# Closed groups of small products, an early split of branch A and sample rows on 128 partitions in a hybrid decoder step

## The chip, the cores and the metric

The kernel runs on one core of a Trainium2 chip. The metric is the device time of one execution in microseconds. Before the change three runs took 897.95, 898.17 and 901.1 us; the median is 898.17 us.

## The reference, cut to what matters

One inference step of a one-layer decoder, for a prompt of 512 rows and for 8 samples of 4 rows each (32 rows). The kernel treats them side by side: 544 columns of rows in all, of which the last 32 are the samples.

```
shift, scale, gate = split(silu(c) @ w_cond + b_cond)
h = x * (1 + scale) + shift
qa, ka, va, za, qkv_b, zb, a_b, b_b, g_a, g_b = split(h @ w_in)
yA = combine(dilated_attention(qa, ka, va, cache_kv, rel_bias)) * silu(za)
yB = rmsnorm(gated_delta(conv(qkv_b), a_b, b_b, state_delta)) * silu(zb)
merged = sigmoid(g_a) * (yA @ w_branch_a) + sigmoid(g_b) * (yB @ w_branch_b)
y = LayerNorm(ALPHA * x + gate * (merged @ w_out)) * ln_g + ln_b
```

Branch A has three head groups (windows 128, 512, 2048 with dilations 1, 4, 16); the samples also attend to caches of 2048 positions. Branch B is the delta rule with a 128x128 state per head, for the samples loaded from `state_delta`. All outputs are f32, the caches and states are returned too.

## The kernel before

Every large product is made in three passes: an operand is split in a rounded high part and the remainder (`hi` and `lo` of the weights, `hhi` and `hlo` of h, `yah` and `yal` of branch A), and hi by hi, lo by hi and hi by lo are summed in PSUM. ACT rounds the high part, DVE subtracts for the low part, PE multiplies. The rows go in two halves of 272 columns, so a job (`Job`: 128 output columns with 8 weight tiles) has 48 matmuls of 272 columns into the PSUM tile `pp`. `stream` runs the jobs one after the other: column jobs of `w_in`, gate jobs (`gate_job`), branch jobs (`branch_job`). The smaller work runs in threads beside it, in the PSUM tiles `pg`, `pd` and `pb`: prompt attention, the delta rule, the sample parts.

The instructions are not issued in the order of the code. A recorder collects them with their dependencies and plans an order for each engine: of what is ready by its cost model, the one with the lowest rank and number goes first; `.at` keeps an instruction back until a time; `rec.together()` makes a group that is issued without another PE instruction between its members, once the operands of all are there. The engines then run in that order. So an edit at one place can move instructions at many others. Each engine's queue is in order: an instruction that waits holds all behind it. SP issues all large DMAs, among them copies of the caches from memory to memory (`out_kv_s`), which stand between the loads.

All instructions are emitted from one line (L725), so the profile is read by names of tiles. The names that the change touches:

- Start: `cond_block` multiplies the conditioning weights `wc` with `cs` (eight products of 32 columns each), copies the sum (`Y`), and with `selc` brings it to features, which gives the scale `sc`. With it `x1h` and `x1l` are made from `xT`, and the first 272-column products (`x1h,hi`) start.
- Sample queries: `sample_queries` transposes the 64 columns of two groups of `qs` for a pair of tiles. T is 0 for the first half of the heads, 1 for the second.
- Sample attention: `sample_attention` makes scores of cache keys (`slab,Qz`; `kv,Qz` for T = 1) and new keys (`ks,Qz`) in `pg`, in products of 32 columns. Its bias comes by DMA as `bias_s` and is changed on ACT (`slab<-slab 128x352`). The same stretch of the program runs the delta rule of the prompt (`U`, `XF`, `W`, `NTs`, `vr`).
- Sample states: `sample_delta` loads for each group G of four heads the states S (8 samples, 512 KB a head) and multiplies each with keys and queries (`KP`), 64 products of 32 columns in a group, G = 0 into `pd` and G = 1 into `pb`. S0 to S3 are those of G = 0, S4 to S7 of G = 1.
- Branch A: `ya` holds attention times silu of za. Its sample columns are written last, by `gate_samples`, after the second sample attention (`od`, `om`, `o`, `os_`). After that the four tiles of 544 columns are split into `yah` and `yal`, and the branch jobs of A start.
- Output: `samples_out` multiplies the merged samples with `w_out` into four blocks of 32 partitions, moves them to one block of 32 rows by 1024 columns, and normalises there; `norm_out` does that for prompt tiles of 128 rows.

Of the kernel before, what the change touches and what calls it, by code (L numbers as in the profile page):

```python
# [19 lines left out]
D = 1024  # L20
# [20 lines left out]
S0B = 7  # L41
TOGETHER = ((0,), (1, 2), (3, 4), (5, 6), (7,))
CHUNKS = ((0, 1), (1, 1), (2, 2), (4, 2), (6, 2))

# [33 lines left out]
def shape_constants():  # L78
# [15 lines left out]
    blk["dmask_s"] = np.where(same & (p[:, None] <= p[None, :]), 0.0, -BIG)  # L94
    blk["bmask"] = (p[:, None] % 32 // 4 == np.arange(8)[None, :])
    blk["hmask"] = (p[:, None] % 4 == np.arange(4)[None, :])
    sab = np.zeros((128, 4, 4))
# [7 lines left out]
    for names in (("ident", "selc", "selg", "low16", "dmask"), ("selab", "sel16", "triu", "btri", "bones"),  # L105
                  ("strict4", "dmask_s", "bmask"), ("hmask",)):
# [671 lines left out]
def body(ctx, tc, io):  # L778
# [27 lines left out]
    def pb_():  # L806
        return psb.tile([128, 512], F32, name="pb", tag="b")
# [85 lines left out]
    with ExitStack() as fctx:  # L893
# [616 lines left out]
    def bias_table(j):  # L1510
# [4 lines left out]
        return bias  # L1515

    dw = dram.tile([2, 4, 2, 4, 128], F32, name="dw")

# [9 lines left out]
    def attention_job(j, g, s):  # L1528
# [4 lines left out]
        def evac(n, ps):  # L1533
            t, scale = pairs[j][s, g], 1.0 if s else -0.125
            if g == 0:
                lo, hi = ((0, 272), (272, 512))[n]
                se.activation(t[:, lo:hi], ps[:, 0:hi - lo], AF.Copy, scale=scale)
            else:
                v = t.rearrange("p (r a n) -> p n a r", r=4, a=4)
                m = (17, 15)[n]  # L1540
                se.activation(v[:, 17 * n:17 * n + m], ps[:, 0:16 * m].rearrange("p (n a r) -> p n a r", a=4, r=4),
                              AF.Copy, scale=scale)
            if n:
                se.activation((qs, ks, vs)[s][:, j, g, :], ps[:, 240:272], AF.Copy, scale=scale)
                if s == 2:
                    threads.set(ready[j, g], 2.5)
# [202 lines left out]
    def sample_attention(T, t, stream, W, pace_of, by, over):  # L1749
# [51 lines left out]
        pS = pg()  # L1801
        for jl in range(2):
            for x in range(1024 // W):
                kt = kts[jl, x]
                for bl in range(0, nb, 2):
                    b = nb * x + bl
                    pe.matmul(pS[16 * b:16 * b + 32, 0:256], Qz[:, 0, jl, 4 * b:4 * b + 8].rearrange("p i h -> p (i h)"),
                              kt[:, 128 * bl:128 * bl + 256], start=(jl == 0), stop=(jl == 1), tile_position=(0, 16 * b))
        for g in range(3):
            for jl in range(2):  # L1810
                for bp in range(4):
                    pe.matmul(pS[32 * bp:32 * bp + 32, 256 + 32 * g:288 + 32 * g],
                              Qz[:, g, jl, 8 * bp:8 * bp + 8].rearrange("p i h -> p (i h)"), ks[:, 2 * T + jl, g, :],
                              start=(jl == 0), stop=(jl == 1), tile_position=(0, 32 * bp))
        ve.tensor_tensor_reduce(Sa, pS[:, 0:352], sb["a"], 1.0, 3e38, op0=OP.add, op1=OP.min, accum_out=sst[:, 0:1])
# [88 lines left out]
    def sample_delta():  # L1904
# [34 lines left out]
        for G in range(2):  # L1939
# [10 lines left out]
            yield 12.0 if G else 6.0  # L1950
            for u in range(2):
                for b in range(8):
                    for h4 in range(4):
                        pe.matmul(pq[32 * h4:32 * h4 + 32, 128 * u:128 * u + 128],
                                  KP[:, u, h4, 32 * b:32 * b + 32], S0[h4][:, b, :],
                                  start=(b == 0), stop=(b == 7 and u == 0), tile_position=(0, 32 * h4))
            rr = rrs[G]
# [326 lines left out]
    ve.memset(eps5, LN_EPS)  # L2284
    r = [o1.tile([128, D], F32, name=f"r{tt}") for tt in range(5)]
    bn = [o1.tile([128, 4 if tt == 3 else 2, 6], F32, name=f"bn{tt}") for tt in range(5)]
# [11 lines left out]
    def load_x(tt, n):  # L2298
        rows = slice(0, 128) if tt < 4 else slice(0, 32)
        xr = o2.tile([128, 512], F32, name="xr")  # L2300
        sp.dma_start(xr[rows], io["x"][128 * tt:128 * tt + 128 if tt < 4 else NT, 512 * n:512 * n + 512])
        se.activation(xr[rows], xr[rows], AF.Copy, scale=ALPHA)
        return xr[rows]

    def norm_out(tt, mv=None):
        rows = slice(0, 128) if tt < 4 else slice(0, 32)
        q = r[tt][rows]
        if mv is None:
            mv = o2.tile([128, 4], F32, name="mv")[rows]
            ve.bn_aggr(mv[:, 0:2], bn[tt][rows].rearrange("p a b -> p (a b)"))  # L2310
        se.activation(mv[:, 2:3], mv[:, 1:2], AF.Sqrt, bias=eps5[rows, 0:1])
        ve.scalar_tensor_tensor(q, q, mv[:, 0:1], lng[rows], op0=OP.subtract, op1=OP.mult)
        ve.reciprocal(mv[:, 2:3], mv[:, 2:3])
        out = io["y_p"][128 * tt:128 * tt + 128] if tt < 4 else io["y_s"]
        for w in (slice(0, 512), slice(512, 1024)):
            ve.scalar_tensor_tensor(q[:, w], q[:, w], mv[:, 2:3], lnb[rows, w], op0=OP.mult, op1=OP.add)
            sp.dma_start(out[:, w], q[:, w])

    def samples_out():
        xr = [load_x(4, n) for n in range(2)]  # L2320
# [7 lines left out]
        q = r[4][0:32]  # L2328
        for b in range(4):
            rows = slice(32 * b, 32 * b + 32)  # L2330
            ve.scalar_tensor_tensor(q[:, 256 * b:256 * b + 256], po[rows, 0:256], 0.5, gs[rows], op0=OP.mult, op1=OP.mult)
        for n in range(2):
            w = slice(512 * n, 512 * n + 512)
            ve.tensor_add(q[:, w], q[:, w], xr[n])
            ve.bn_stats(bn[4][0:32, n, :], q[:, w])
        norm_out(4)

# [56 lines left out]
def lay_out(x):  # L2394
# [12 lines left out]
        "const_d": CONST[2],  # L2407
        "const_s": CONST[3],
        "x": rows,
        "xT": rows.T.reshape(KT, 128, NT).transpose(1, 0, 2),  # L2410
# [60 lines left out]
```

## Time and profile before

| | us |
|---|---|
| median of three runs | 898.17 |
| profiled execution, whole | 902.66 |
| its span | 900.9 |
| PE busy | 873.6 |
| DVE busy | 650.8 |
| ACT busy | 449.9 |
| POOL busy | 74.1 |

The mean granted clock of TensorE is 0.993. The queue of the large transfers is busy 76.3% of the span. Where rows of the profile or the timeline are shown, a tile's name is followed by what it is made of (`pp<-hhi,hi`: into `pp` from `hhi` and `hi`), PEld is the weight load that runs beside PE, SPq is the time in which SP issues a DMA, and `128*32` is the part of the array that a product uses (rows by columns). An f32 product that is not rounded runs in two passes and shows as two instructions.

### The profile page before, as it was taken

The page shows a single profiled execution, that of the slowest core. Times are in us where ns is not written, and L with a number is a line of the kernel's source. Part 1 is how long each engine was busy: PE and PEld are TensorE (multiplying, and loading weights), DVE is VectorE, ACT ScalarE, POOL GpSimd, SP SyncE. Part 2 cuts the span into 40 slices and gives each one's busy share as a digit, 9 for nine tenths or more (in the row PEclk, how much of TensorE's full clock was granted, in tenths as well). Part 3 has the DMA queues.
Part 4 walks back from the last instruction along what each step waited for, and adds up shares of the span by engine and source line. Part 5 has one row for each costly group of instructions (what it writes and reads, how often), then busy time and mean ns, then how long its engine had stood idle before and what let it go on. Part 6 is the DMA issues. An engine that isn't in the chain of part 4 may idle for free.

```text
span 900.9 us, 20727 instructions
## 1 busy us (share of the span) xinstructions
PE 873.6 (97%) x8178; PEld 822.2 (91%) x8178; DVE 650.8 (72%) x1341; ACT 449.9 (50%) x1076; POOL 74.1 (8%) x173
## 2 busy tenths in 40 slices
PE   6999999999999999999999999999999999989995
PEld 5899999898899999899999899897999999989884
DVE  3675447643379998399987658366889698978568
ACT  3555478733478834579734565642542222324331
POOL 0120011100101200012101101020010000001000
PEclk9999999999999999999999999999999999999998
DMA  9865785785868798878889556559869799985953
GB/s 348 322 212 172 235 277 174 249 275 165 293 200 302 234 293 276 309 245 261 274 287 286 188 193 214 177 180 317 315 224 382 270 408 411 352 305 170 366 187 122
DMA packets 106189, 235.84 MB, mean 262 GB/s; under 512 B 30199, under 2 KB 61633, under 8 KB 103405
## 3 DMA queue, kind: packets, MB, share of 16 engines
q1 hardware_dynamic: 106092, 234.53, 76.3%
q8 instruction: 64, 1.05, 0.5%
q14 instruction: 33, 0.26, 0.1%
HBM read 218.20 MB, written 103.97 MB: 358 GB/s over the span
## 4 chain that ended last, share of the span: by engine, by line
PE 83%; DVE 7%; ACT 4%; DMA 4%; issue 1%; SPq 1%; DVEq 0%; ACTq 0%
PE pp L725 63%; PE pg L725 9%; PE pd L725 7%; PE pb L725 4%; DVE slab L725 1%; ACT L725 1%; DMA S<-in_state_delta 1%; DVE lo L725 1%; DMA rbo<-dO 1%; DVE acc L725 1%; DVE r L725 1%; DMA slab<-in_bias_s 1%; SPq L725 1%; DMA out_kv_s<-in_cache 1%; DMA wc<-in_w_cb 1%
## 5 line engine op out<-in xcount | busy, mean ns | idle before, releaser
L725 PE MATMUL pp<-hhi,hi 128*128 128x272 f32 x1360 | 400.8, 295 | 1.0 <-DVE zt L725 0.5
L725 PE MATMUL pp<-hlo,hi 128*128 128x272 f32 x1360 | 400.8, 295 | 0.0
L725 PE MATMUL pp<-hhi,lo 128*128 128x272 f32 x1360 | 399.9, 294 | 0.0
L725 PEld LDWEIGHTS pp<-hhi,hi 128*128 128x128 f32 x1360 | 256.8, 189 | 4.8 <-issue 2.2
L725 PEld LDWEIGHTS pp<-hhi,lo 128*128 128x128 f32 x1360 | 256.6, 189 | 3.8 <-issue 2.7
L725 PEld LDWEIGHTS pp<-hlo,hi 128*128 128x128 f32 x1360 | 257.1, 189 | 2.8 <-issue 1.7
L725 ACT ACTIVATE hi<-wt 128x1024 fp32r<-128x1024 f32 (+1 forms) x101 | 103.6, 1026 | 160.3 <-PE pp L725 135.1
L725 DVE TENSOR_TENSOR lo<-wt,hi 128x1024 fp32r<-128x1024 f32 (+1 forms) x101 | 119.0, 1178 | 81.3 <-ACT hi L725 74.5
L725 DVE SCALAR_TENSOR_TENSOR acc<-ext,cw,acc 128x568 f32<-128x568 f32 x72 | 57.9, 804 | 0.8 <-ACT acc L725 0.2
L725 DVE TENSOR_TENSOR slab<-slab 128x512 f32<-128x512 f32 (+1 forms) x66 | 43.3, 670 | 10.0 <-DMA slab<-qd 4.4
L725 ACT ACT_TABLE_LOAD x32 | 41.1, 1283 | 5.2 <-PE pp L725 3.0
L725 DVE TENSOR_REDUCE slab<-slab 128x8 f32<-128x512 f32 (+2 forms) x66 | 42.8, 660 | 0.3
L725 ACT ACTIVATE zt<-pp 128x272 f32<-128x272 f32 x48 | 18.8, 391 | 40.6 <-PE pp L725 38.4
L725 ACT ACTIVATE P<-P,st 128x256 f32<-128x256 f32 (+1 forms) x64 | 31.3, 493 | 12.7 <-DVE st L725 12.6
L725 PE MATMUL pp<-ybh,lo 128*128 128x272 f32 x128 | 37.0, 289 | 0.0
L725 PE MATMUL pp<-ybl,hi 128*128 128x272 f32 x128 | 37.0, 289 | 0.0
L725 PE MATMUL pp<-ybh,hi 128*128 128x272 f32 x128 | 36.8, 288 | 0.0
L725 POOL COPY cx<-ext 128x3 f32<-128x3 f32 (+1 forms) x48 | 23.9, 527 | 114.5 <-ACT ext L725 109.9
L725 DVE CUSTOM_DVE_ANT_0 P<-pg,bias 128x256 f32<-128x256 f32 (+1 forms) x64 | 23.1, 401 | 9.3 <-PE pg L725 9.1
L725 ACT ACTIVATE spare<-pp 128x272 f32<-128x272 f32 (+1 forms) x32 | 16.2, 505 | 19.8 <-PE pp L725 18.2
L725 PEld LDWEIGHTS pp<-ybh,hi 128*128 128x128 f32 x128 | 24.2, 189 | 0.1
L725 PEld LDWEIGHTS pp<-ybl,hi 128*128 128x128 f32 x128 | 24.1, 188 | 0.1
(402 smaller groups left out, 1574.5 us busy)
## 6 DMA issues: line engine op xcount, KB each, us to landing
out_kv_s<-in_cache SPq DMA_DIRECT2D x144, 512.0 KB
wt<-in_w_in SPq DMA_DIRECT2D x85, 512.0 KB
out_kv_s<-in_cache SPq DMA_DIRECT2D x24, 496.0 KB
wc<-in_w_cb SPq DMA_DIRECT2D x16, 512.0 KB
slab<-in_ks SPq DMA_DIRECT2D x32, 256.0 KB
slab<-in_vs SPq DMA_DIRECT2D x32, 256.0 KB
kv<-in_ks SPq DMA_DIRECT2D x16, 512.0 KB
kv<-in_vs SPq DMA_DIRECT2D x16, 512.0 KB
```

What stands on the lines that cost most here:

```text
L725: getattr(real[x.engine], x.name)(*map(arg, x.args), **{k: arg(v) for k, v in x.kw.items()})
```

## The change

It has six parts.

1. At the start, `cond_block` for the first chunk of the scale issues products of `ones` with itself: 8 ahead of its group, 2 behind it, 5 behind the product with `selc`. Nothing reads them. The next chunk's group is kept back until 9.9 us.
2. The three groups of `qs` are stored in rotated order (`at_g`), so that the transposition takes 96 columns from the start of the tile; the first 64 rows of the result are used as before.
3. The scores of the first sample attention and the products of the states of G = 0 become closed groups.
4. The prompt columns of `ya` are split by a thread, `split_prompt_a`, which starts when the fourth job from the end of the gate jobs is over; at the border only the 32 sample columns are split, straight from `os_`.
5. The sample rows stay on 128 partitions (four blocks of 256 columns), with `ln_g` and `ln_b` loaded so (`lns`); the mean and the mean square over the four blocks come from two products with a constant matrix (`quarter`).
6. By all this the planned order differs in many places.

```diff
+IDLE = (8, 2, 5)
...
+    blk["quarter"] = np.where(p[:, None] % 32 == p[None, :] % 32, 0.25, 0.0)
...
+            idle = IDLE if (part, at) == (1, 0) else (0, 0, 0)
             rec.rank = -1
+
+            def turn_over(n):
+                for _ in range(n):
+                    pe.matmul(ps[:, 384:512], ones, ones, start=True, stop=True)
+
+            turn_over(idle[0])
             with rec.together():
                 for k in range(KT):
                     q = k % 4
                     pe.matmul(ps[32 * q:32 * q + 32, 0:w].rearrange("p (a b) -> p a b", b=128), cs[:, k, :], wc[:, :, k, :],
-                              start=(k < 4), stop=(k >= 4), tile_position=(0, 32 * q))
+                              start=(k < 4), stop=(k >= 4), tile_position=(0, 32 * q)).at = 9.9 * ((part, at) == (1, 1))
+                turn_over(idle[1])
...
+                turn_over(idle[2])
...
+    at_g = lambda g: (g + 2) % 3
...
-            pe.transpose(pt[0:64, 0:128], qs[:, 2 * T + jl, 1:3].rearrange("p g n -> p (g n)"), ident).at = GATES[1] + 12.0
+            pe.transpose(pt[0:96, 0:128], qs[:, 2 * T + jl].rearrange("p g n -> p (g n)"), ident).at = GATES[1] + 12.0
...
+        with rec.together() if not T else nullcontext():
...
         for j in range(4):
-            ve.tensor_copy(ya[j][:, SEQ:], os_[:, j])
+            se.activation(yah[j][:, SEQ:], os_[:, j], AF.Copy)
+            ve.tensor_sub(yal[j][:, SEQ:], os_[:, j], yah[j][:, SEQ:].bitcast(F32))
+
+    def split_prompt_a():
+        yield split_at.over
+        for j in range(4):
+            yah[j] = keep.tile([128, NT], F32R, name="yah", tag="ya", bufs=5)
+            se.activation(yah[j][:, :SEQ], ya[j][:, :SEQ], AF.Copy)
+            yal[j] = op.tile([128, NT], F32R, name="yal", tag="o")
+            ve.tensor_sub(yal[j][:, :SEQ], ya[j][:, :SEQ], yah[j][:, :SEQ].bitcast(F32))
+            yield 6.0
...
+            with rec.together() if not G else nullcontext():
...
+    split_at = jobs[-4]
...
+    threads.add(split_prompt_a(), 0)
...
-    for j in range(4):
-        yah[j] = keep.tile([128, NT], F32R, name="yah", tag="ya", bufs=5)
-        se.activation(yah[j], ya[j], AF.Copy)
-        yal[j] = op.tile([128, NT], F32R, name="yal", tag="o")
-        ve.tensor_sub(yal[j], ya[j], yah[j].bitcast(F32))
...
+        q = r[4]
+        ve.scalar_tensor_tensor(q, po[:, 0:256], 0.5, gs, op0=OP.mult, op1=OP.mult)
+        ve.tensor_add(q, q, xr)
+        ve.bn_stats(bn[4][:, 0, :], q)
+        mv = o2.tile([128, 4], F32, name="mv")
+        ve.bn_aggr(mv[:, 0:2], bn[4][:, 0, :])
+        pm = pd()
+        pe.matmul(pm[:, 0:1], quarter, mv[:, 0:1], start=True, stop=True)
+        se.activation(mv[:, 2:3], pm[:, 0:1], AF.Square, bias=mv[:, 0:1], scale=-1.0)
+        ve.tensor_add(mv[:, 1:2], mv[:, 1:2], mv[:, 2:3])
+        pe.matmul(pm[:, 1:2], quarter, mv[:, 1:2], start=True, stop=True)
```

What stands on ACT at the first sample attention, before (`slab<-slab 128x352` is the copy that waits for `bias_s`; `U` and `XF` are operands of the delta rule):

```order
L725 ACTIVATE W<-pd 32x256 x2
L725 ACTIVATE k<-pp 128x17x4x4
L725 ACTIVATE U<-pd 32x8x32
L725 ACTIVATE XF<-pd 32x8x32 x2
L725 ACTIVATE hi<-wt 128x1024
L725 ACTIVATE k<-pp 128x15x4x4
L725 ACTIVATE ks<-pp 128x32
L725 ACTIVATE slab<-slab 128x352
L725 ACTIVATE U<-pd 64x512
```

The same place of ACT in the changed kernel:

```order
L727 ACTIVATE k<-pp 128x17x4x4
L727 ACTIVATE W<-pd 32x256 x2
L727 ACTIVATE slab<-slab 128x352
L727 ACTIVATE U<-pd 32x8x32
L727 ACTIVATE XF<-pd 32x8x32
L727 ACTIVATE hi<-wt 128x1024
L727 ACTIVATE k<-pp 128x15x4x4
L727 ACTIVATE ks<-pp 128x32
L727 ACTIVATE XF<-pd 32x8x32
L727 ACTIVATE slab<-slab 128x256
L727 ACTIVATE U<-pd 64x512
```

The copy of the slab has moved ahead of `U<-pd 32x8x32`, and the second `U` now stands behind the other slab's copy.

What stands in SP's queue at the loads of the states, before (the names carry the numbers of their buffers, S0 first; `wt` is a raw weight tile):

```order
L725 DMA S_8424<-in_state_delta 128x8x128
L725 DMA S_8426<-in_state_delta 128x8x128
L725 DMA S_8430<-in_state_delta 128x8x128
L725 DMA S_8433<-in_state_delta 128x8x128
L725 DMA wt<-in_w_in 128x1024
L725 DMA S_8465<-in_state_delta 128x8x128
L725 DMA S_8473<-in_state_delta 128x8x128
L725 DMA S_8487<-in_state_delta 128x8x128
L725 DMA S_8496<-in_state_delta 128x8x128
```

The same place of SP in the changed kernel:

```order
L727 DMA S_8422<-in_state_delta 128x8x128
L727 DMA S_8425<-in_state_delta 128x8x128
L727 DMA S_8433<-in_state_delta 128x8x128
L727 DMA S_8441<-in_state_delta 128x8x128
L727 DMA S_8446<-in_state_delta 128x8x128
L727 DMA S_8468<-in_state_delta 128x8x128
L727 DMA S_8486<-in_state_delta 128x8x128
L727 DMA wt<-in_w_in 128x1024
L727 DMA S_8518<-in_state_delta 128x8x128
```

The weight tile has moved from behind S3 to behind S6. On PE the order behind the group of G = 0 in the changed kernel is this (S4, S5 and S6 are the first three heads of G = 1):

```order
L727 MATMUL pd<-S_8433,KP 32x128
L727 MATMUL pd<-S_8441,KP 32x128
L727 MATMUL pb<-S_8446,KP 32x128
L727 MATMUL pb<-S_8468,KP 32x128
L727 MATMUL pb<-S_8486,KP 32x128
L727 MATMUL pp<-hlo,hi 128x272
L727 MATMUL pp<-hhi,lo 128x272
```

Before, it was this:

```order
L725 MATMUL pd<-S_8433,KP 32x128
L725 MATMUL pb<-S_8465,KP 32x128
L725 MATMUL pb<-S_8473,KP 32x128
L725 MATMUL pp<-hhi,hi 128x272
L725 MATMUL pp<-hlo,hi 128x272
L725 MATMUL pp<-hhi,lo 128x272
```

The product of S6 has moved from behind thirteen pp products to directly behind that of S5.

More of the change, by code (lines that the diff above doesn't have):

```diff
@@ L105, in shape_constants @@
     for names in (("ident", "selc", "selg", "low16", "dmask"), ("selab", "sel16", "triu", "btri", "bones"),
-                  ("strict4", "dmask_s", "bmask"), ("hmask",)):
+                  ("strict4", "dmask_s", "bmask"), ("hmask",), ("quarter",)):
         at = 0
@@ L1543, in evac @@
             if n:
-                se.activation((qs, ks, vs)[s][:, j, g, :], ps[:, 240:272], AF.Copy, scale=scale)
+                se.activation((qs, ks, vs)[s][:, j, g if s else at_g(g), :], ps[:, 240:272], AF.Copy, scale=scale)
                 if s == 2:
@@ L1801, in sample_attention @@
         pS = pg()
[L1802 to L1809, printed above, removed]
-            for jl in range(2):
[L1811 to L1814, printed above, removed]
+        with rec.together() if not T else nullcontext():
+            for jl in range(2):
+                for x in range(1024 // W):
+                    kt = kts[jl, x]
+                    for bl in range(0, nb, 2):
+                        b = nb * x + bl
+                        pe.matmul(pS[16 * b:16 * b + 32, 0:256], Qz[:, at_g(0), jl, 4 * b:4 * b + 8].rearrange("p i h -> p (i h)"),
+                                  kt[:, 128 * bl:128 * bl + 256], start=(jl == 0), stop=(jl == 1), tile_position=(0, 16 * b))
+            for g in range(3):
+                for jl in range(2):
+                    for bp in range(4):
+                        pe.matmul(pS[32 * bp:32 * bp + 32, 256 + 32 * g:288 + 32 * g],
+                                  Qz[:, at_g(g), jl, 8 * bp:8 * bp + 8].rearrange("p i h -> p (i h)"), ks[:, 2 * T + jl, g, :],
+                                  start=(jl == 0), stop=(jl == 1), tile_position=(0, 32 * bp))
         ve.tensor_tensor_reduce(Sa, pS[:, 0:352], sb["a"], 1.0, 3e38, op0=OP.add, op1=OP.min, accum_out=sst[:, 0:1])
@@ L1950, in sample_delta @@
             yield 12.0 if G else 6.0
[L1951 to L1956, printed above, removed]
+            with rec.together() if not G else nullcontext():
+                for u in range(2):
+                    for b in range(8):
+                        for h4 in range(4):
+                            pe.matmul(pq[32 * h4:32 * h4 + 32, 128 * u:128 * u + 128],
+                                      KP[:, u, h4, 32 * b:32 * b + 32], S0[h4][:, b, :],
+                                      start=(b == 0), stop=(b == 7 and u == 0), tile_position=(0, 32 * h4))
             rr = rrs[G]
@@ L2284, in body @@
     ve.memset(eps5, LN_EPS)
-    r = [o1.tile([128, D], F32, name=f"r{tt}") for tt in range(5)]
+    lns = o1.tile([128, 2, 256], F32, name="lns")
+    for i, n in enumerate(("ln_g", "ln_b")):
+        for q in range(4):
+            sp.dma_start(lns[32 * q:32 * q + 32, i], io[n][:, 256 * q:256 * q + 256].to_broadcast([32, 256]))
+    quarter = o1.tile([128, 128], F32, name="quarter")
+    sp.dma_start(quarter, io["const_q"])
+    r = [o1.tile([128, D if tt < 4 else 256], F32, name=f"r{tt}") for tt in range(5)]
     bn = [o1.tile([128, 4 if tt == 3 else 2, 6], F32, name=f"bn{tt}") for tt in range(5)]
@@ L2298, in load_x @@
     def load_x(tt, n):
-        rows = slice(0, 128) if tt < 4 else slice(0, 32)
         xr = o2.tile([128, 512], F32, name="xr")
-        sp.dma_start(xr[rows], io["x"][128 * tt:128 * tt + 128 if tt < 4 else NT, 512 * n:512 * n + 512])
-        se.activation(xr[rows], xr[rows], AF.Copy, scale=ALPHA)
-        return xr[rows]
+        sp.dma_start(xr, io["x"][128 * tt:128 * tt + 128, 512 * n:512 * n + 512])
+        se.activation(xr, xr, AF.Copy, scale=ALPHA)
+        return xr
     def norm_out(tt, mv=None):
-        rows = slice(0, 128) if tt < 4 else slice(0, 32)
-        q = r[tt][rows]
+        q = r[tt]
         if mv is None:
[L2309 to L2312, printed above, removed]
+            mv = o2.tile([128, 4], F32, name="mv")
+            ve.bn_aggr(mv[:, 0:2], bn[tt].rearrange("p a b -> p (a b)"))
+        se.activation(mv[:, 2:3], mv[:, 1:2], AF.Sqrt, bias=eps5)
+        ve.scalar_tensor_tensor(q, q, mv[:, 0:1], lng, op0=OP.subtract, op1=OP.mult)
         ve.reciprocal(mv[:, 2:3], mv[:, 2:3])
-        out = io["y_p"][128 * tt:128 * tt + 128] if tt < 4 else io["y_s"]
         for w in (slice(0, 512), slice(512, 1024)):
-            ve.scalar_tensor_tensor(q[:, w], q[:, w], mv[:, 2:3], lnb[rows, w], op0=OP.mult, op1=OP.add)
-            sp.dma_start(out[:, w], q[:, w])
+            ve.scalar_tensor_tensor(q[:, w], q[:, w], mv[:, 2:3], lnb[:, w], op0=OP.mult, op1=OP.add)
+            sp.dma_start(io["y_p"][128 * tt:128 * tt + 128, w], q[:, w])
     def samples_out():
-        xr = [load_x(4, n) for n in range(2)]
+        xr = o1.tile([128, 256], F32, name="xs")
+        for b in range(4):
+            sp.dma_start(xr[32 * b:32 * b + 32], io["x"][SEQ:NT, 256 * b:256 * b + 256])
+        se.activation(xr, xr, AF.Copy, scale=ALPHA)
         po = pp()
@@ L2327, in samples_out @@
                               start=(k == 0), stop=(k == 7), tile_position=(0, 32 * q))
-        q = r[4][0:32]
-        for b in range(4):
[L2330 to L2336, printed above, removed]
+        q = r[4]
+        ve.scalar_tensor_tensor(q, po[:, 0:256], 0.5, gs, op0=OP.mult, op1=OP.mult)
+        ve.tensor_add(q, q, xr)
+        ve.bn_stats(bn[4][:, 0, :], q)
+        mv = o2.tile([128, 4], F32, name="mv")
+        ve.bn_aggr(mv[:, 0:2], bn[4][:, 0, :])
[4 more added lines that the diff above has]
+        pe.matmul(pm[:, 1:2], quarter, mv[:, 1:2], start=True, stop=True)
+        se.activation(mv[:, 3:4], pm[:, 1:2], AF.Sqrt, bias=eps5)
+        ve.tensor_copy(mv[:, 2:3], pm[:, 0:1])
+        ve.scalar_tensor_tensor(q, q, mv[:, 2:3], lns[:, 0], op0=OP.subtract, op1=OP.mult)
+        ve.reciprocal(mv[:, 3:4], mv[:, 3:4])
+        ve.scalar_tensor_tensor(q, q, mv[:, 3:4], lns[:, 1], op0=OP.mult, op1=OP.add)
+        for b in range(4):
+            sp.dma_start(io["y_s"][:, 256 * b:256 * b + 256], q[32 * b:32 * b + 32])
     for n in range(2):
@@ L2408, in lay_out @@
         "const_s": CONST[3],
+        "const_q": CONST[4],
         "x": rows,
```

## The prediction

> **What bounds the kernel now.** I read the page first: span, busy shares, then the shares of the chain that ended last.
>
> ```profile
> span 900.9 us, 20727 instructions
> PE 873.6 (97%) x8178; PEld 822.2 (91%) x8178; DVE 650.8 (72%) x1341; ACT 449.9 (50%) x1076; POOL 74.1 (8%) x173
> PE 83%; DVE 7%; ACT 4%; DMA 4%; issue 1%; SPq 1%; DVEq 0%; ACTq 0%
> ```
>
> PE is busy 97% of the span and carries 83% of the chain. So time is gained only where PE stands still, runs at a lower clock, or loses time between matmuls of different shape, and every wait that PE newly gets costs its full length. I then listed the idle stretches of PE in the timeline and tabulated the three places that matter most (columns: length, busy time of PE, PEld, DVE, ACT, POOL, then granted clock, DMA share, GB/s).
>
> ```profile
> 237.00:247.00 10.00, 8.56 (x64) 8.28 (x63) 3.30 (x7) 3.38 (x7) 0.30 (x1) 0.83 0.95 350
> 780.00:800.00 20.00, 20.00 (x162) 20.00 (x161) 19.63 (x18) 4.89 (x10) 0.00 (x0) 1.00 0.94 342
> 804.00:814.00 10.00, 7.14 (x36) 5.98 (x35) 5.80 (x15) 4.18 (x7) 0.00 (x0) 0.83 0.56 171
> ```
>
> A clock of 0.83 over 10 us is 3.4 us at half speed, (1 - 0.83) x 10 / 0.5. It loses 1.7 us of work. Both such stretches stand right behind a wait of PE (1.44 us at 240.4 and 2.09 us at 806.7, rows below). So I charge 1.7 us to each new wait of that length.
>
> **The start.** Times of the timeline are start, duration, engine, operation, and in brackets the idle time before it.
>
> ```profile
> 8.11 0.70 ACT L725 ACTIVATE x1h<-xT,sc 128x512 fp32r<-128x512 f32 x1
> 9.08 1.08 PE L725 MATMUL pb<-wc,cs 128*32 128x128 f32 x16 [1.84 <-DMA wc<-in_w_cb]
> 12.95 0.43 PE L725 MATMUL pd<-x1h,lo 128*128 128x272 f32 x1
> 13.18 0.43 PE L725 MATMUL pd<-x1l,hi 128*128 128x272 f32 x1
> 13.82 0.29 PE L725 MATMUL pg<-x1h,lo 128*128 128x272 f32 x1
> 13.94 0.29 PE L725 MATMUL pg<-x1h,hi 128*128 128x272 f32 x1
> ```
>
> A 272-column matmul starts every 0.23 us until 13.7 and every 0.12 us from there: the clock turns full only there. Between 10.09 and 13.7 fifteen such matmuls run, each 0.10 us slower than later: 1.5 us. The change fills PE with 15 products of a tile of ones: 8 from the moment `ones` is set, where PE waits for weights, 2 and 5 in the gaps behind. If that brings the full clock before 10 us, 1.5 us go. The two products ahead of the `selc` product delay the scale `sc` by under 0.4 us; x1h starts at 8.11 only because ACT is then free, so most of that is hidden. Ends: nothing (DMA sets the pace instead) and 1.9 us. I take -1.5 us.
>
> **Closed groups and the query transposes.** First the transposes, now 96 columns instead of 64.
>
> ```profile
> 216.81 0.27 PE L725 MATMUL pg<-cst,qs 128*64 128x128 f32 x1
> ...
> 217.05 0.29 PE L725 MATMUL pp<-hhi,lo 128*128 128x272 f32 x1
> ...
> 236.91 0.27 PE L725 MATMUL pg<-cst,ks 128*96 128x128 f32 x1
> ...
> 237.14 0.29 PE L725 MATMUL pp<-hlo,hi 128*128 128x272 f32 x1
> ```
>
> From the transposition to the second pp matmul behind it 0.24 us pass with 64 columns, and 0.23 us with 96. So this edit is worth nothing: 0. [...] At 32 columns it is different:
>
> ```profile
> 619.08 0.28 PE L725 MATMUL pp<-hlo,hi 128*128 128x272 f32 x1
> 619.29 0.41 PE L725 MATMUL pd<-S,KP 128*32 128x128 f32 x2
> 619.62 0.39 PE L725 MATMUL pp<-hhi,lo 128*128 128x272 f32 x1
> 619.85 0.29 PE L725 MATMUL pp<-hhi,hi 128*128 128x272 f32 x1
> ...
> 622.37 3.57 PE L725 MATMUL pd<-S,KP 128*32 128x128 f32 x121
> ```
>
> From 619.08 to 619.85 are 0.77 us, of which the two pp matmuls need 0.25: the single product (two passes) costs 0.52 us. Inside the group two passes cost 3.3 / 60 = 0.055 us. Three singles (617.8, 619.3, 620.8) join the group: 3 x 0.47 = 1.4 us. The score products of the first sample attention stood in four clusters, two of them here:
>
> ```profile
> 381.02 0.25 PE L725 MATMUL pg<-ks,Qz 128*32 128x32 f32 x2
> ...
> 382.70 0.56 PE L725 MATMUL pg<-ks,Qz 128*32 128x32 f32 x40
> ```
>
> Now one: three clusters at between 0.2 and 0.47 us; I take 1.0. Together -2.4 us (ends -1.6 and -2.8).
>
> **What the closed S group brings behind it.** The rows of SP in the part on the change show four loads of the state, wt, four loads; after it seven, wt, one. The rows of PE show the products of S4, S5 and S6 now right behind the group.
>
> ```profile
> 626.54 0.41 PE L725 MATMUL pb<-S,KP 128*32 128x128 f32 x2 [0.48 <-DMA S<-in_state_delta]
> ...
> 629.74 0.41 PE L725 MATMUL pb<-S,KP 128*32 128x128 f32 x2 [0.74 <-DMA S<-in_state_delta]
> ```
>
> Before, S6 came at 629.7, and PE put 13 pp matmuls into the time between. With wt behind S6 it lands some 1.4 us sooner, at 628.3; PE asks for it at about 625.9 and, as nothing stands between, waits 2.4 us. Behind it queue all later matmuls. Against 1.5 us lost now (two waits with their turns, 0.74 each): +0.9, and with the half clock that follows such a wait +1.7. I take +2.5 us (ends -0.7, if S6 lands with S5, and +3.5).
>
> **bias_s.** With other costs of the instructions around it, the order at the first sample attention is planned anew.
>
> ```profile
> 228.69 2.41 SPq L725 DMA_DIRECT2D out_kv_s<-in_cache  x2
> ...
> 231.60 0.66 ACT L725 ACTIVATE k<-pp 128x272 f32<-128x272 f32 x1
> 233.64 0.38 ACT L725 ACTIVATE U<-pd 32x256 f32<-32x256 f32 x1 [1.38 <-PE pd L725]
> ...
> 239.21 0.50 ACT L725 ACTIVATE slab<-slab 128x352 f32<-128x352 f32 x1 [2.50 <-DMA slab<-in_bias_s]
> ...
> 235.48 1.14 PE L725 MATMUL pd<-U,NTs 64*64 64x64 f32 x16
> ...
> 240.37 1.14 PE L725 MATMUL pd<-XF,U 64*64 64x64 f32 x16 [1.44 <-ACT U L725]
> ```
>
> ACT's copy of the bias slab waits for its load until 239.21 and holds `U<-pd 64x512` behind it, for which PE waits 1.44 us. In the change this copy stands five instructions earlier, ahead of `U<-pd 32x8x32`, which PE needs for pd<-U,NTs at 235.48. One of the two cache copies ahead of the load is gone from SP's queue (1.2 us of its issue time), so the slab comes at some 237.3 to 238; then slab 0.5 us, U 0.38 us, and PE starts at about 238.2 instead of 235.5. That is a wait of 2.7 us in place of 1.44, followed by the half clock as now; pd<-XF,U then finds its operand in time. +1.2 us (ends: the load comes as ACT asks, -3.2 with the half clock gone; no earlier than now, +2.6).
>
> [...]
>
> **Early split of branch A.**
>
> ```profile
> 802.76 0.42 DVE L725 TENSOR_TENSOR om<-pg,od 128x256 f32<-128x256 f32 x1 [1.95 <-PE pg L725]
> ...
> 806.02 0.66 ACT L725 ACTIVATE yah<-ya 128x544 fp32r<-128x544 f32 x1 [0.67 <-DVE ya L725]
> ...
> 806.71 0.73 DVE L725 TENSOR_TENSOR yal<-ya,yah 128x544 fp32r<-128x544 f32 x1 [0.47 <-ACT yah L725]
> 806.73 0.52 PE L725 MATMUL pp<-yah,hi 128*128 128x272 f32 x2 [2.09 <-ACT yah L725]
> ```
>
> At the border four copies, four splits on ACT and four on DVE stand one after the other, and PE follows at their pace: window 804 to 814 has 2.86 us without PE and 1.7 us lost by the clock, 4.6; by the distances of matmul starts, which see the smaller delays too, 5.6. Now the 512 prompt columns are split while gate jobs run, and the border keeps 32 columns of four tiles. I take 5.2 back. The cover: DVE gets four subtractions of 128x512; `lo<-wt 128x512` is the nearest shape (0.68 us, the next instruction 0.60 behind it), 2.4 us in all. DVE is full from 780 to 800 (19.63 of 20.00); cover is the 0.37 us there and the 1.95 us before om. So om comes up to 0.3 us late, and with it the sample columns. -4.9 us (ends -3.5 and -5.6). ACT has 15 us free there.
>
> **Sample output.**
>
> ```profile
> 868.11 0.41 DVE L725 SCALAR_TENSOR_TENSOR r<-pp,gs 32x256 f32<-32x256 f32 x1 [1.84 <-PE pp L725]
> ...
> 890.38 0.29 PE L725 MATMUL pp<-wo1h,mlo 128*128 128x256 f32 x1
> ...
> 890.73 0.41 DVE L725 SCALAR_TENSOR_TENSOR r<-pp,gp 128x256 f32<-128x256 f32 x1
> ```
>
> DVE waits for PE here (1.84 us), and at the end it starts 0.35 us behind PE's last matmul: what the 128-partition form saves on DVE lies beside PE. The order behind the last matmul is the same, so the 10 us from there to the end stay. Added on PE are two one-column products, each at most two passes like the transposes above (0.11 us a pass), with waits that later products cover: +0.3 us (ends 0 and +1.0). More small loads stand in SP's queue ahead of xr, which DVE and not PE would feel.
>
> **The sum.** -1.5 - 2.4 + 2.5 + 1.2 - 4.9 + 0.3 = -4.8 us on a span of 900.9. The profiled execution took 902.66 us, 1.8 more than its span and 4.5 more than the median of the runs; I put the difference on the median 898.17: 893.4 us.
>
> **Rivals.**
> 1. The two waits are half as bad, since S6 and bias_s land earlier than I read from the rows: halfway to the ends named above (2.5 to -0.7 and 1.2 to -3.2) is -4.8 - 1.6 - 2.2 = -8.6: 889.6. For it: one copy fewer ahead of bias_s. Against: SP can't issue the load before 231. Chance 0.20.
> 2. The waits come but the clock stays full: 1.7 us less at S6 and 1.7 at bias_s, -8.2: 890. Against it are both 0.83 rows. Chance 0.05. [...]
> 3. The change doesn't do all it says: the ones don't help because loads, not the clock, pace the start (0 instead of -1.5), and of the split only the first wait goes because DVE, full until 800, delivers the samples late (-3 instead of -4.9): -1.4: 896.8. For it: DVE's 19.63 of 20. Chance 0.20.
> 4. Slower: ACT stands at the bias slab while SP's queue is deeper than before. Each us that the slab lands later than 237.5 costs PE one, as U and then every product of the delta rule are behind it. From a landing at 242.3, 4.8 us later than I take, all gains are gone; at 247 the time is 903. For it: DMA is busy 0.95 there. Against: a copy less is ahead. Chance 0.08.
>
> **Chances and range.** The forecast has 0.47, by itself 891 to 896. 0.5% is 4.5 us, about what a measurement of this kernel can tell from no change; the forecast lies on that edge, so a little over half of it counts as faster (0.27). With rivals 1 and 2 (0.25) that is 0.52. Rival 3, the rest of the forecast: same 0.39, with a hundredth of rival 4. Slower 0.09. The range takes in rivals 1 to 3: 888.5 to 899.
>
> **What would show it.** Start: 272-column matmuls 0.12 us apart before 10 us. S group: one wait of 2 to 3 us at the third pb<-S,KP, none before. bias_s: a wait before pd<-U,NTs instead of pd<-XF,U. Split: no wait at the first pp<-yah, clock 1.00 there. Wrong would be: no wait at S6 (then lower), or waits of lo<-wt between 780 and 800 (then higher).

## The result, and the profile after

Four runs of the changed kernel, the profiled one among them, have a median of 891.41 us (890.0 to 893.03); the kernel before, with one more run than above, has 899.5 us (four runs, 897.95 to 901.1). The ratio is 0.9893, with a 95% interval of 0.9866 to 0.992: faster by 0.8 to 1.3%. The two medians alone give 0.991, inside that interval. The profiled execution took 891.03 us. Head and chain of its page:

```profile
span 889.1 us, 20805 instructions
PE 868.8 (98%) x8212; PEld 821.2 (92%) x8212; DVE 646.1 (73%) x1338; ACT 453.9 (51%) x1083; POOL 70.0 (8%) x173
...
PE 89%; ACT 3%; DMA 2%; DVE 2%; SPq 1%; issue 1%; DVEq 0%; ACTq 0%
```

PE carries 89% of the chain instead of 83%, and it was idle in gaps for 9.0 us instead of 16.7 (gaps over 0.15 us, up to its last product). Of these 7.8 us, 4.1 lie ahead of PE's first product, which starts at 1.05 us instead of 5.16 because the useless products fill the time; behind it 11.6 us of idle time became 7.9.

**How two traces are compared here.** Both kernels run the same 5136 large products (272, 512 or 256 columns: those into `pp`, and those of x1) on PE, in the same order but for 29 places at the start and at the split of branch A. I read when the nth of them starts in each trace; the difference stays constant within 0.1 us where nothing differs, and steps where something does. Where small products stand in another order it can jump for a few products: at 3300 it moves by 0.9 us within two products, so each of the two rows that meet there is sure only to that, while their sum is surer. As I took a second trace of both kernels (below), the steps are means of two executions each, before minus after:

| products | place | step, us | forecast, us |
|---|---|---|---|
| 1 to 100 | start | +1.3 | +1.5 |
| to 2000 | bias slab | +1.8 | -1.2 |
| to 2500 | scores of the first sample attention | +2.5 | +1.0 |
| to 3300 | waits at 540 us | -3.1 | 0 |
| to 4500 | products of the states | +5.0 | -1.1 |
| to 4700 | split of branch A | +5.6 | +4.9 |
| to 5100 | products for the sample output | -0.4 | -0.3 |
| to the end | tail | -0.9 | 0 |
| sum | | +11.8 | +4.8 |

The two profiled executions of before lie above its median, so 11.8 is more than the 8.1 us between the medians; the shares are what counts here, and one of them, the bias slab's, turns out below to belong to the single executions.

**Start.** From the timeline of the changed kernel:

```profile
1.05 0.58 PE L727 MATMUL pg<-ones 128*128 128x128 f32 x1 [1.05 <-DVE ones L727]
5.00 0.76 PE L727 MATMUL pg<-wc,cs 128*32 128x128 f32 x16 [0.17 <-DMA wc<-in_w_cb]
...
11.21 0.29 PE L727 MATMUL pd<-x1l,hi 128*128 128x272 f32 x1
11.34 0.29 PE L727 MATMUL pd<-x1h,lo 128*128 128x272 f32 x1
...
19.02 0.85 PE L727 MATMUL pb<-wc,cs 128*32 128x256 f32 x12 [1.40 <-DMA wc<-in_w_cb]
```

PE is busy from 1.05 us, and the 272-column products start 0.12 to 0.13 us apart as soon as they run in a row; before, this spacing came only at 13.7 us. At 17.6 PE has caught up with the loads of `wc` and waits 1.40 us for one.

**Bias slab.** The same view at the first sample attention:

```profile
229.69 1.01 SPq L727 DMA_DIRECT2D slab<-in_bias_s  x2
...
233.87 0.50 ACT L727 ACTIVATE slab<-slab 128x352 f32<-128x352 f32 x1 [2.33 <-DMA slab<-in_bias_s]
234.40 0.38 ACT L727 ACTIVATE U<-pd 32x256 f32<-32x256 f32 x1
...
235.68 1.14 PE L727 MATMUL pd<-U,NTs 64*64 64x64 f32 x16
...
238.89 1.14 PE L727 MATMUL pd<-XF,U 64*64 64x64 f32 x16
```

ACT stands 2.33 us at the slab, ahead of U as forecast, but the slab is there at 233.87 and U in time: no bracket stands behind pd<-U,NTs. The load was issued 2.7 us sooner than before (229.69 against 232.40), and it took 4.2 us instead of 6.8 to the copy on ACT.

**540 us.** Nothing of the change touches this place. Here PE, ACT and DVE of the changed kernel:

```profile
537.03 0.69 ACT L727 ACTIVATE kq<-pb,small 128x512 f32<-128x512 f32 x1
537.74 1.28 ACT L727 ACT_TABLE_LOAD   x1
539.03 0.40 ACT L727 ACTIVATE spare<-pp 128x272 f32<-128x272 f32 x1
539.45 1.28 ACT L727 ACT_TABLE_LOAD   x1
540.74 0.20 ACT L727 ACTIVATE rn<-rn 128x4 f32<-128x4 f32 x1
540.97 1.28 ACT L727 ACT_TABLE_LOAD   x1
...
537.75 3.35 DVE L727 RECIPROCAL kq<-kq 128x512 f32<-128x512 f32 x1 [1.84 <-ACT kq L727]
541.02 0.38 DVE L727 SCALAR_TENSOR_TENSOR spare<-spare,pp 128x272 f32<-128x272 f32 x1
...
541.46 0.39 PE L727 MATMUL pp<-hhi,hi 128*128 128x272 f32 x1 [1.54 <-DVE spare L727]
...
543.82 0.66 PE L727 MATMUL pb<-cst,uv 128*128 128x128 f32 x4 [0.83 <-ACT crow L727]
```

```profile
538.98 0.21 ACT L725 ACTIVATE rn<-rn 128x4 f32<-128x4 f32 x1 [0.23 <-DVE rn L725]
539.19 0.69 ACT L725 ACTIVATE kq<-pb,small 128x512 f32<-128x512 f32 x1
...
540.90 1.28 ACT L725 ACT_TABLE_LOAD   x1
542.42 0.40 ACT L725 ACTIVATE spare<-pp 128x272 f32<-128x272 f32 x1 [0.24 <-PE pp L725]
```

The second fence is the timeline of before. There both square roots (`rn`, `kq`) stood side by side, and one table load followed. Now `spare`, which needs another table, stands between them: behind the root of `kq` come three loads of 1.28 us where one was (36 on the page, 32 before). DVE's multiply for `spare`, which frees the PSUM that PE needs, stands behind a 3.35 us reciprocal. PE waits 1.54 and 0.83 us.

**States and split.** Timeline of the changed kernel at the products of the states, and at the first branch products of A:

```profile
604.73 12.49 SPq L727 DMA_DIRECT2D S<-in_state_delta  x7
...
617.96 3.70 PE L727 MATMUL pd<-S,KP 128*32 128x128 f32 x128
...
622.04 0.41 PE L727 MATMUL pb<-S,KP 128*32 128x128 f32 x2 [0.18 <-DMA S<-in_state_delta]
...
796.95 0.37 PE L727 MATMUL pp<-yah,hi 128*128 128x272 f32 x1
```

And of before, PE's wait for `rbo` (loaded by DMA) ahead of these products, and the issue of the last four states:

```profile
616.23 0.66 PE L725 MATMUL pg<-cst,rbo 128*128 128x128 f32 x4 [1.03 <-DMA rbo<-dO]
...
619.18 5.83 SPq L725 DMA_DIRECT2D S<-in_state_delta  x4
```

The third pb<-S,KP waits 0.18 us, not 2.4. The first pp<-yah has no wait, where before stood 2.09 us. The windows view over 10 us at these places (columns as in the prediction):

```profile
540.00:550.00 10.00, 7.38 (x63) 6.43 (x64) 7.85 (x23) 6.04 (x13) 0.34 (x1) 1.00 0.62 196
...
797.00:807.00 10.00, 10.00 (x81) 10.00 (x80) 8.15 (x20) 4.65 (x11) 1.12 (x2) 1.00 0.61 188
```

PE is full behind the split, at clock 1.00 (7.14 of 10 at 0.83 before). At 540 it loses 2.6 us, at clock 1.00 as well.

**Output and tail.** Timeline of the changed kernel:

```profile
857.05 0.28 PE L727 MATMUL pd<-mv,quarter 128*128 128x1 f32 x2
...
877.68 0.29 PE L727 MATMUL pp<-wo1h,mlo 128*128 128x256 f32 x1
...
875.15 0.42 DVE L727 SCALAR_TENSOR_TENSOR r<-pp,gp 128x256 f32<-128x256 f32 x1 [0.52 <-PE pp L727]
875.49 0.74 DVE L727 SCALAR_TENSOR_TENSOR r<-r,mv,lnb 128x512 f32<-128x512 f32 x1
...
876.49 0.75 DVE L727 SCALAR_TENSOR_TENSOR r<-r,mv,lnb 128x512 f32<-128x512 f32 x1
...
878.81 0.41 DVE L727 SCALAR_TENSOR_TENSOR r<-pp,gp 128x256 f32<-128x256 f32 x1
```

PE's last product starts at 877.68 and DVE takes it 1.13 us later, where before 0.35 us passed (890.38 to 890.73). Between DVE's last two r<-pp stand two operations with `lnb` now, and one before: 0.74 us of DVE more in front of the last piece.

### The profile page after: what moved, and what is told of

The parts are those of the page before. It is cut to its first block, busy times and chain, and to the rows that moved or that the text cites. A ratio compares the mean times of both kernels' runs of the same rounds, so it can differ in the third digit from the quotient of the medians.

```text
span 889.1 us, 20805 instructions
## 1 busy us (share of the span) xinstructions
PE 868.8 (98%) x8212; PEld 821.2 (92%) x8212; DVE 646.1 (73%) x1338; ACT 453.9 (51%) x1083; POOL 70.0 (8%) x173
## 3 DMA queue, kind: packets, MB, share of 16 engines
q8 instruction: 64, 1.05, 0.5%
## 4 chain that ended last, share of the span: by engine, by line
PE 89%; ACT 3%; DMA 2%; DVE 2%; SPq 1%; issue 1%; DVEq 0%; ACTq 0%
PE pp L727 68%; PE pg L727 9%; PE pd L727 8%; PE pb L727 4%; DMA wc<-in_w_cb 2%; SPq L727 1%; ACT L727 1%; DVE r L727 1%; DMA S<-in_state_delta 1%; ACT sq L727 1%; ACT hi L727 0%; DVE lo L727 0%; DVE zt L727 0%; ACT ext L727 0%; ACT acc L727 0%
```

## The experiments

The theory behind them: each step of the table has its own cause, at its own place. Its rivals: a step is scatter of single executions, or comes from the new order as a whole. All are compared in the way above, most with `after`. For each I give the median, with the range and the number of runs, and the ratio to the kernel before with its interval.

### Both kernels once more (after_again, before_again)

No edit.

> The changed kernel once more, unaltered, for a second trace and more times. In traces of other kernels with its order the wait at pd<-U,NTs behind the bias slab is 0 to 1.7 us and the one for S6 0 to 1.0 us. Theory, that these waits belong to single executions: this trace differs from the first by 0.5 to 2.5 us in the stages with loads (the first 100, 1200 to 1400, 3300 to 3700) and by under 0.1 us in the others; the median stays between 890 and 893 us. Rival, that they belong to the edits of those kernels: all stages agree within 0.3 us.

> The kernel before once more, unaltered, for a second trace. Theory, that its wait at pd<-XF,U (1.44 us and half clock behind) belongs to single executions: it is absent here, as in the kernel with the early split alone, or differs by over 1 us; the 2.1 us at the border of branch A and the half clock behind it stay, as no load decides them. Rival, that the wait at pd<-XF,U belongs to the order: it is here again within 0.3 us.

The changed kernel: 891.62 us (890.27 to 892.28, 5), ratio 0.9889 [0.9872, 0.9905]. Its two traces agree within 0.1 us everywhere but at the load of `wc` (0.92 us less; the wait at 17.5 is 0.74 instead of 1.40), in the bias stage (0.58 less), at the delta rule behind it (0.31 more) and at the states (0.44 less). The kernel before took 901.3 us. Its second trace waits 0.58 us instead of 1.44 before pd<-XF,U, and the wait at the split stays (2.09 us); the mean granted clock of this execution is 0.994, that of the first was 0.993. So the large waits between engines that no load stands behind (1.54, 0.83 and 2.09 us) repeat to a hundredth or two, and what hangs on loads changes by some 0.5 to 2 us from one execution to the next.

### The early split alone (split_alone)

The kernel before with part 4 of the change only (`split_prompt_a` and the two lines of `gate_samples`, as in the diff above).

> The kernel before with the early split of branch A and nothing else; the order on PE differs in 8 places, all behind the 4590th large product. Theory: between the 4500th and 4700th large product 5.0 to 5.8 us go (2.9 us without PE, 1.7 us of half clock, about 1 us of small delays), the median falls by about 5.5 us. Rival, that DVE, full until 800, gives part back: 3 us or less.

Measured: 897.9 us (895.96 to 899.49, 10), ratio 0.9967 [0.9952, 0.9982], so 3.2 us, where some 5.5 were expected. On PE 5.0 us go at the split. What is left there is one wait:

```profile
805.15 0.36 PE L725 MATMUL pp<-yah,hi 128*128 128x272 f32 x1 [0.49 <-ACT yah L725]
...
885.09 0.41 DVE L725 SCALAR_TENSOR_TENSOR r<-pp,gp 128x256 f32<-128x256 f32 x1
```

This timeline also shows the tail: PE's last product starts at 883.26, DVE takes it 1.83 us later, and the span ends 1.5 us later behind PE's last product than before. So the longer tail comes with the new order of DVE, without the new output code. Of the 5.0 us on PE 3.5 reach the end.

### The products of ones at 4 columns (tiny_ones)

The order of all instructions is the same; the 15 products are 4 columns wide instead of 128, and the planner is told their old cost.

```diff
-                    pe.matmul(ps[:, 384:512], ones, ones, start=True, stop=True)
+                    d = pe.matmul(ps[:, 384:388], ones, ones[:, 0:4], start=True, stop=True)
+                    rec.now += 0.224 - d.cost
+                    d.cost = 0.224
```

> The changed kernel with the fifteen products of ones 4 columns wide instead of 128, in the same places: every other instruction stands in the same order on every engine. Theory, that they work by keeping PE busy so that the clock turns full sooner: the full clock comes at 10 to 14 us instead of 5 to 7, and PE is 0.6 to 2.0 us later at its 100th large product (the range in which executions of the changed order differ there). Rival, that the load of wc at 17 to 19 us sets the pace of the start anyway: within 0.3 us at the 100th product.

```profile
14.68 0.43 PE L727 MATMUL pg<-x1l,hi 128*128 128x272 f32 x1
14.90 0.43 PE L727 MATMUL pg<-x1h,lo 128*128 128x272 f32 x1
...
15.33 0.29 PE L727 MATMUL pg<-x1l,hi 128*128 128x272 f32 x1
15.46 0.29 PE L727 MATMUL pg<-x1h,lo 128*128 128x272 f32 x1
```

In its timeline the products start 0.23 us apart until 15.1 us: without PE being full, the clock is late as in the kernel before. The 100th large product comes 1.30 us later than in `after`, and 2.1 us later than in `after_again`. 893.86 us (892.55 to 897.08, 6), ratio 0.993 [0.9909, 0.9951]. So the start's gain is the clock, and nothing else of the start.

### Groups left open (open_s, open_q)

```diff
-            with rec.together() if not G else nullcontext():
+            with nullcontext():
```

This is open_s, the states; open_q does the same at the scores (`if not T`).

> The changed kernel with the products of the states of G = 0 not closed. Between its 3300th and 4500th large product the changed kernel won 4.8 us. Theory: the single products cost 1.4 us (three at 0.47), and the waits for rbo and S went because their loads are issued some 3.8 us sooner, which this edit leaves: 1.0 to 1.6 us come back. Rival, that the closed group itself takes the waits away: 4 to 5 us come back.

> The changed kernel with the score products of the first sample attention not closed. Between its 2000th and 2500th large product the changed kernel won 2.6 us. Theory, that a cluster of 32-column products costs two turns wherever it stands: 1.0 to 1.5 us of it come back, the rest was a wait for XF that another order took away. Rival, that the closed group makes all of it: 2.6 us.

open_s: 893.27 us (892.3 to 897.15, 6), ratio 0.993 [0.9908, 0.9953]. From product 3300 to 3700 it loses 1.65 us, and gets 0.75 back until 4500. By the distances from start to start, the products of G = 0 take 4.32 us there instead of 3.52, and the large products 0.85 more. No product waits for a state or for `rbo`. So closing the group is worth 0.9 to 1.65 us, as forecast, and the rest of the 5.0 us is not from it. About 2 us of that rest are the waits of before for `rbo` and S: 2.25 us in one trace of before and 1.75 in the other, against 0.18 and none in those of the changed kernel. They are gone with the group open too, which fits loads that are issued sooner; no run changed the loads alone. What is left, 1 to 2 us, was not traced.

open_q: 899.58 us (896.55 to 902.92, 10), ratio 0.9987 [0.9967, 1.0007]. Behind the scores it is 3.1 us later than `after`, 1.0 of it in waits.

The groups view of before, over the 17 us around the scores (count, busy time, mean ns), and below it that of `after`:

```profile
L725 PE MATMUL pg<-ks,Qz 128*32 128x32 f32 x48 | 1.3, 200 | 0.0
```

```profile
L727 PE MATMUL pg<-ks,Qz 128*32 128x32 f32 x48 | 0.7, 199 | 0.0
```

The same 48 products keep PE 1.3 us in clusters and 0.7 us in a group. I added up the distances from start to start by kind, for the large products 2001 to 2100 and what lies between them: all score products take 2.27 us in before and in open_q, 1.48 in `after`; the hundred large products, which also pay for what stands ahead of them, 14.91, 15.16 and 14.19. So of the 2.5 us of this step 0.8 + 0.7 = 1.5 come from closing the group. Another 0.5 is a wait at pd<-XF,W, 0.53 and 0.50 us in the two traces of before, none and 0.12 in those of the changed kernel; the rest is spread over products that stand in another order. The new order of open_q also removed the waits at 540 (3.5 us better) and lost 8.6 us behind, among others in waits of 1.31 us for S and of 1.06, 2.50 and 1.32 for tiles of the sample states (`vns`, `orow`, `vx`), and at a lower clock: behind the wait of 2.50 us pd<-us,sel x8 takes 1.91 us, against 1.04 in q64.

### The old sample output (old_out)

Part 5 undone: `samples_out` with one block of 32 rows, without `quarter`.

```diff
-        pe.matmul(pm[:, 0:1], quarter, mv[:, 0:1], start=True, stop=True)
...
+            rows = slice(32 * b, 32 * b + 32)
+            ve.scalar_tensor_tensor(q[:, 256 * b:256 * b + 256], po[rows, 0:256], 0.5, gs[rows], op0=OP.mult, op1=OP.mult)
```

> The changed kernel with the sample output as before, on 32 rows of 1024 columns. In the changed kernel PE loses 0.4 us at the two one-column products, and DVE starts on PE's last product 0.85 us after its start instead of 0.35, the end is 0.9 us further from it. Theory, that both belong to the output edit: 1.2 to 1.4 us faster than the changed kernel. Rival, that only the 0.4 us on PE do: 0.4 us faster. My forecast of 0.3 us would be right with the rival.

890.2 us (889.07 to 893.55, 4), ratio 0.9885 [0.9853, 0.9917]. PE gains 0.41 us exactly where the two one-column products were, as the rival has it; the tail is 0.6 us longer than in `after`, not shorter. So part 5 is worth nothing that these runs can tell. Up to there the order on PE is that of `after`, and still this execution waits 1.07 us before pd<-U,NTs and 1.04 us for S6: scatter of loads again.

### Query transposes at 64 columns (q64, q64_same)

```diff
-            pe.transpose(pt[0:96, 0:128], qs[:, 2 * T + jl].rearrange("p g n -> p (g n)"), ident).at = GATES[1] + 12.0
+            pe.transpose(pt[0:64, 0:128], qs[:, 2 * T + jl, 0:2].rearrange("p g n -> p (g n)"), ident).at = GATES[1] + 12.0
```

In q64 the planner is free; in q64_same it is told the old form and place, and the order stays that of `after`.

> The changed kernel with the query transposes back at 64 columns (the rotated order of the groups stays). By that the planner puts ACT's copy of the bias slab behind ks again, and two cache copies ahead of its load, as in the kernel before. Theory, that the cache copy ahead of the load sets when the slab lands: PE waits about 1.4 us at pd<-XF,U, the clock halves behind it, and PE is 2.4 to 3.2 us later at its 2000th large product than in the changed kernel. First rival, that the load came early because all was 0.6 us ahead: under 0.7 us later. Second rival, that a 64-column transpose drains the array: 0.3 to 0.4 us lost at each of the four transposes.

> The changed kernel with the query transposes at 64 columns and every instruction in the place of the changed kernel. Theory, that 64 and 96 columns cost PE the same: under 0.05 us at each of the four transposes. Rival, that 64 columns drain the array: 0.2 to 0.4 us at each.

q64_same: 891.2 us (one run); from a transposition to the second product behind it 0.24 us pass, with 96 columns 0.24. Width costs nothing here. q64: 896.26 us (894.5 to 901.82, 10), ratio 0.9965 [0.9946, 0.9984]: 4.9 us slower than `after` by the medians, from another order alone. Its timeline:

```profile
236.02 0.50 ACT L727 ACTIVATE slab<-slab 128x352 f32<-128x352 f32 x1 [0.69 <-DMA slab<-in_bias_s]
...
237.49 1.14 PE L727 MATMUL pd<-XF,U 64*64 64x64 f32 x16
...
648.97 0.59 PE L727 MATMUL pp<-hhi,hi 128*128 128x272 f32 x1 [3.63 <-DVE zt L727]
```

ACT has the old order at the slab, the slab is there at 236.02, and PE doesn't wait; at its 2000th large product it is 1.4 us earlier than in `after`. So the theory fails, and with 0.24 us behind a transposition here too, so does the second rival: the wait of before was one of landing, not of the place of the copy. q64 loses its time at 645 us, in a wait of 3.63 us for `zt`, the copy that frees `pp`; behind it the 272-column products start 0.23 us apart until 650.5, where ahead of it 0.12 to 0.13 us passed.

### The waits at 540 (recip4, rn_kq)

recip4 cuts the long reciprocal in four; rn_kq keeps both square roots of that head back to the same time.

```diff
-        ve.reciprocal(kqf, kqf)
+        for u in range(4):
+            ve.reciprocal(kqf[:, u // 2, 128 * (u % 2):128 * (u % 2) + 128], kqf[:, u // 2, 128 * (u % 2):128 * (u % 2) + 128])
```

```diff
-        se.activation(rn, rn, AF.Sqrt)
+        se.activation(rn, rn, AF.Sqrt).at = 529.0 * (h == 6)
-        se.activation(kqf, ps.rearrange("p (s n) -> p s n", s=2), AF.Sqrt, bias=eps4[:, 0:1])
+        se.activation(kqf, ps.rearrange("p (s n) -> p s n", s=2), AF.Sqrt, bias=eps4[:, 0:1]).at = 529.0
```

> The changed kernel with the reciprocal of kq (128x512, 3.35 us on DVE) in four pieces, so that spare's product can stand between them. Theory, that the wait of 1.54 us for spare at 540 us is DVE's long reciprocal: that wait goes, 1.3 to 1.7 us faster at the 3000th large product; the wait of 0.83 us behind it (ACT, table loads) stays. Rival, that ACT's four table loads make both: no change.

> The changed kernel with the square roots of kq and rn side by side on ACT, so that two of its 36 table loads go (the order around 540 us differs a little on all engines). Theory, that table loads set the wait of 0.83 us and help to set that of 1.54 us: 1 to 2.7 us faster at the 3000th large product. Rival, that only DVE's reciprocal does: 0 to 0.8 us faster.

The windows view of recip4, and then of rn_kq:

```profile
530.00:550.00 20.00, 19.97 (x159) 18.22 (x158) 15.16 (x43) 16.19 (x43) 0.87 (x2) 1.00 0.60 193
```

```profile
530.00:550.00 20.00, 20.00 (x166) 18.54 (x165) 14.24 (x39) 14.30 (x39) 1.67 (x2) 1.00 0.65 187
```

Both remove the waits there (`after` has 17.30 of 20 us busy; rn_kq has one of 0.78 us for `spare` at 555 instead) and gain 3.9 and 4.1 us on PE up to product 3200, more than either forecast. recip4 does it with 36 table loads still, rn_kq with 34. So the wait takes both causes, and either cure helps, as far as two kernels show it whose order is planned anew from there on. Neither kernel is faster in the end: 896.53 us (894.33 to 900.28, 9), ratio 0.996 [0.9941, 0.9979], and 893.69 us (892.35 to 896.75, 6), ratio 0.9934 [0.9914, 0.9955]. The order behind is planned anew in both, and the next stage loses 6.1 and 7.4 us: in recip4 waits of 1.19, 0.98 and 1.16 us, in rn_kq a wait of 2.02 us for S6 and one of 2.67 us for `zt`. The mean granted clock of both is 0.993, against 0.996 in `after`.

```profile
625.64 0.41 PE L727 MATMUL pb<-S,KP 128*32 128x128 f32 x2 [2.02 <-DMA S<-in_state_delta]
```

This row of the timeline of rn_kq is the wait that the prediction had put into the changed kernel, at the place it named. No version that I ran beats the changed kernel beyond the intervals.

## Why the prediction came out as it did

The direction and the range were right; the size was not. I forecast -4.8 us on a median of 898.17, that is 893.4; measured were 891.41, and against the kernel before beside it -8.1 and, in a later session, -9.9 us. That the time lies in the range is in part luck: scores, slab and states came out 10.6 us better than forecast in the traces, and the waits at 540 and the tail, which stood at nothing, took 4.0 of that back. By the steps:

- **Start**, -1.5: -1.3 (0.6 and 2.1 in the two pairs of traces). Right, and tiny_ones shows its cause. What the clock gave, a load of `wc` takes back in part: 1.40 us in one execution, 0.74 in the next.
- **Transposes**, 0: 0, by q64_same.
- **Scores**, -1.0: -2.5. The term was too small. Closing the group is worth 1.5: I had priced three clusters at 0.33 us each, and the large products beside them lose nearly as much again. With it went a wait of 0.5 us on the delta rule, which I hadn't looked for.
- **Singles of the states**, -1.4: -0.9 to -1.65 by open_s. Right.
- **Wait at S6**, +2.5: 0 to +1.0 in the five traces with this order (0.18 in `after`, none in `after_again` and tiny_ones, 0.84 in q64_same, 1.04 in old_out); in `after` the granted clock from 615 to 640 us was 1.00. This is the step that failed. I moved S6's landing only by the one weight tile that it had passed, 1.4 us. But the whole queue ran sooner: S6's issue ran from 615.83 to 617.23, and from 620.90 to 623.52 before; with the 2.6 us that PE is ahead at that place, it ended 3.7 us sooner against PE's products. PE asked at 621.86 and S6 was there at 622.04. The waits of before went too, 1.03 us for `rbo` and 0.48 and 0.74 for S in the first trace; the prediction had counted the S waits as gained, but had no term for `rbo`. So the stage gained 5.0 us, where I had a loss of 1.1.
- **Bias slab**, +1.2: -1.8. The place was right: ACT stands at the slab ahead of U, and where the slab is late, PE waits before pd<-U,NTs (1.07 us in old_out, 1.14 in rn_kq, 0.92 in tiny_ones). The size was taken from one landing of one execution. Over the traces this stage runs between 0.6 us better and 2.4 us worse than `after` in the new order, and between 0.7 better and 2.3 worse in the old one: it belongs to the single execution. On average the nine traces of the new order are 0.7 us worse there than `after` and the four of the old order 0.5, so the change as such gains nothing in this stage, and the -1.8 is luck of the two pairs. Without it the steps add up to 10.0 us, near the 8.1 and 9.9 between the medians. The load was issued at 229.69, though I had held that SP could not do so before 231.
- **Split**, -4.9: -5.6, and -5.0 alone. Right in mechanism and nearly in size: the first pp<-yah waits in neither trace of the changed kernel.
- **Output**, +0.3: +0.4 on PE. Right.
- **Tail**, 0: +0.9. Wrong: DVE's last steps stand in another order, with one operation of 0.74 us more ahead of the last piece. It comes with the early split alone too, so not from the output code. That this operation is the whole of it was read from the rows, not tried.
- **Not foreseen**: the waits at 540, +3.1. Two square roots drifted apart in the plan. They stand apart in q64 and in open_q too, and PE waits 1.52 us in q64, but 0.18 in open_q, where the root of `kq` came sooner (534.60). Which part of the change moved them was not tried. The order of the changed kernel shows it, but I compared orders only at the places that the diff names.

Rival 1 (889.6) came nearest in mechanism: both waits were shorter than read from the rows. Rival 2 (890), waits but full clock, came nearest in time. The clock of `after` did stay at 1.00 at both places (230 to 240 and 615 to 640 us), but the waits of 2.4 and 2.7 us that this rival keeps were not there; and where waits did come, at 540, the last section shows 1.00 behind them in two executions and 0.50 in two others. Rival 3 fell: start and split did all they were to do. Rival 4 fell too, with a slab at 233.87.

## What to carry to other kernels

Take a second trace of the same kernel before pricing a wait on a load: here such waits changed by 0.5 to 2 us between executions, while the large waits between engines alone repeated to 0.02. In a planned kernel look through the new order for what the diff doesn't name, above all for functions with different tables that drift apart on ACT (a load took 1.28 us here) and for long instructions ahead of short ones that free a buffer (3.35 us ahead of 0.38). And price a cluster of narrow products together with what the wide ones beside it lose (here 0.8 and 0.7 us), not by its own length.

## What the hardware showed that I had not expected

**Behind the same waits the clock was full in some executions and half in others.** The two waits at 540 (1.54 and 0.83 us in `after`) are 1.5 and 0.8 us long in after_again, tiny_ones and old_out too. In tiny_ones the granted clock behind them is 0.50, by the windows view:

```profile
547.75:551.17 3.42, 3.17 (x19) 2.59 (x20) 3.23 (x9) 0.65 (x4) 0.00 (x0) 0.50 0.67 210
```

In old_out it is 0.50 as well (544 to 547 us). In `after` it is 1.00 from 540 to 550 us, as the row under States and split shows, and in after_again 1.00 from 539 to 548. So the 1.7 us that I charged behind each wait was an estimate from the two waits of before (1.44 and 2.09 us, a clock of 0.83 over 10 us at both): behind these it came, behind the waits at 540 only in some executions. What decides it was not shown.

**Useless products buy clock.** Filling PE from 1.05 us on gave full clock between 4.3 and 7.0 us in the nine traces with these products at full width, against 13.7 to 15.3 in the four without them (tiny_ones, with products of 4 columns, is one of the four). The 16 passes of pb<-wc,cs at 9 us take 0.65 us in `after` and 1.08 in before.
